# Six modulation pieces of four columns in place of twelve of two, in the attention of an encoder layer

## The chip, the cores and the metric

The kernel runs on one core of a Trainium2 chip. The metric is the device time of one execution, in microseconds (us); lower is better. PE is the matmul engine, PEld its weight load, DVE the vector engine, ACT the scalar engine, POOL the GpSimd engine; SP only issues DMAs.

## The reference

One encoder layer on x (1024 tokens, 1024 features), float32. A vector c conditions it:

```python
mod = (silu(c) @ w_ada + b_ada)            # 1024 -> 6 * 1024
sh1, sc1, g1, sh2, sc2, g2 = split(mod, 6)
h = rmsnorm(x, norm_g[0]) * (1 + sc1) + sh1
y = hybrid_mixer(h, ...)                   # three attentions A, B, C; 24 gates; output projection
x = x + g1 * rmsnorm(y, norm_g[1])
h = rmsnorm(x, norm_g[2]) * (1 + sc2) + sh2
x = x + g2 * rmsnorm(conv_ffn(h), norm_g[3])
```

The mixer has four heads for each of A (chunked), B (forgetting) and C (sparse, the best 256 keys of an indexer). Each attention's result is projected to 1024 features and multiplied by a sigmoid gate, `sigmoid(h @ w_in[:, gate columns] + b_gate)`, before the sum.

## The kernel before, in words

`mod` is kept as 48 columns of 128 values. Columns 0 to 15 (sh1, sc1) are made at the start, 40 to 47 (g2) at the end; the change touches neither. Columns 16 to 39 (g1, sh2, sc2) are first used when the attention is over; they are made meanwhile, in *pieces*.

A piece of two columns (`ada_load`, `ada_piece`): two DMAs (line 185) bring 1024 x 256 weights in two blocks of 512 KB. DVE makes c-weighted sums of the eight 128x256 slices into `ada_acc`, in two accumulators that take turns (2 instructions of line 196, 6 of line 198). POOL adds the two accumulators (line 204). PE sums over the partitions, one fp32 matmul of width 1 for each column (line 208; the trace shows each as two), into a PSUM bank of tag `d`. DVE makes two columns of `mod` out of the bank (line 210). `ada_acc` has one buffer.

The attention (lines 842 to 940) is a loop over 12 heads, each of four groups of two query blocks: PE makes scores, DVE adds a bias and takes maxima (line 762), ACT takes exponentials (772), POOL scales by the reciprocals of the sums (777), PE transposes (811), ACT and DVE split the result (816, 817), PE weighs the values (800, 801). Beside it, DVE and ACT search the thresholds of C's keys: 31 rounds of counting (`select_keys`, 647 to 668), and after them the masks (691 to 698), which C's first head needs.

The gates and pieces are *filler* for PE: `items` is a list that `tick` advances while the attention is written down, at a priority 100 lower. A gate (`m_tile`) loads 512 KB of weights (line 238, a `raw` buffer), splits them into a high and a low part (231 on ACT, 232 on POOL), runs 48 matmuls (247 to 249) into two banks of tag `d`, and evacuates each by ACT (530). There are two `d` banks, for gates and pieces alike, three `raw` buffers (`N_RAW`) of 512 KB for the weights of gates and of pieces, and four buffers for split weights, enough for two gates. 20 of the 24 gates are items; `ADA_AT` says behind which of them a piece stands. `run_all` calls the loads of item n+1 just before the steps of item n.

Nobody writes the order of the attention by hand: a planner simulates the engines' times and puts the instructions into each engine's queue by priority and readiness, past the written order where buffers allow. On the chip each engine then goes through its queue in that order.

Of the kernel before, what the change touches and what calls it, by code (L numbers as in the profile page):

```python
# [7 lines left out]
F32 = mybir.dt.float32  # L8
# [4 lines left out]
OP = mybir.AluOpType  # L13
# [3 lines left out]
P = 128  # L17
S = 1024
D = 1024
KD = D // P  # L20
# [10 lines left out]
HAND_FROM = 11  # L31
N_HELD = 2
LATE_M = (1, 3, 5, 7)
ADA_AT = (1, 2, 3, 4, 5, 6, 7, 8, 11, 13, 15, 17)
RELOAD = (1, 3, 5)
BB = "s"
N_F4 = 2
# [23 lines left out]
def encoder_layer(ctx: ExitStack, tc: tile.TileContext, x, w_ada, w_in, w_branch, w_out, w_up, w_down,  # L61
                  vec_a, vec_c, rel_pad, b_forget, cos_t, sin_t, out):
    nc = tc.nc
    act = nc.scalar
    dve = nc.vector
    pool = nc.gpsimd
    pe = nc.tensor
# [7 lines left out]
    small = ctx.enter_context(tc.tile_pool(name="small", bufs=4))  # L75
# [16 lines left out]
    def raw4(name, shape=(P, 1024), dt=F32):  # L92
        return rawp.tile(list(shape), dt, tag="raw", name=name, bufs=N_RAW)
# [13 lines left out]
    def bank(tag, name):  # L107
        return psum.tile([P, HALF], F32, tag=tag, name=name, bufs=N_BANKS[tag])
# [33 lines left out]
    one = const.tile([P, 1], F32, name="one")  # L142
# [19 lines left out]
    c_act = const.tile([P, KD], F32, name="c_act")  # L162
# [5 lines left out]
    mod = const.tile([P, 48], F32, name="mod")  # L168
    mod_b1 = const.tile([P, 48], F32, name="mod_b1")
# [3 lines left out]
    mod_g = const.tile([P, 48], F32, name="mod_g")  # L173
# [4 lines left out]
    def ada_load(srcs, alloc):  # L178

        wv = w_ada.rearrange("(k p) c -> p k c", p=P)  # L180
        raw = [alloc(f"ada_raw{g}", (P, 4, 2, P)) for g in range(2)]
        for g in range(2):
            ks_ = slice(4 * g, 4 * g + 4)
            if srcs[1] == srcs[0] + 1:
                nc.sync.dma_start(raw[g].rearrange("p k t c -> p k (t c)"), wv[:, ks_, srcs[0] * P:(srcs[0] + 2) * P])
            else:
                for j, u in enumerate(srcs):
                    nc.sync.dma_start(raw[g][:, :, j, :], wv[:, ks_, u * P:(u + 1) * P])
        return [raw[k // 4][:, k % 4] for k in range(KD)]

    def ada_steps(per_k):

        acc = small.tile([P, 2, 2, P], F32, tag="ada_acc", name="ada_acc", bufs=1)
        for k in range(KD):
            if k < 2:
                dve.tensor_scalar(acc[:, k], per_k[k], c_act[:, k:k + 1], None, op0=OP.mult)
            else:
                dve.scalar_tensor_tensor(acc[:, k % 2], per_k[k], c_act[:, k:k + 1], acc[:, k % 2],  # L198
                                         op0=OP.mult, op1=OP.add)
            yield acc  # L200

    def ada_end(srcs, acc, tag="n", eng=pool, pm=None):

        eng.tensor_tensor(acc[:, 0], acc[:, 0], acc[:, 1], op=OP.add)
        if pm is None:
            pm = bank(tag, "ada_ps")
        for j, t in enumerate(srcs):
            pe.matmul(pm[:, j:j + 1], acc[:, 0, j], one, start=True, stop=True)
        for j, t in enumerate(srcs):
            last = dve.scalar_tensor_tensor(mod[:, t:t + 1], pm[:, j:j + 1], mod_b1[:, t:t + 1],  # L210
                                            mod_g[:, t:t + 1], op0=OP.add, op1=OP.mult)
        return last

    def ada_piece(srcs, per_k, tag="n", pm=None):
        for acc in ada_steps(per_k):
            pass
        ada_end(srcs, acc, tag, pool, pm)
# [122 lines left out]
    with tc.manual_schedule(engines={E.Activation, E.DVE, E.Pool, E.PE}):  # L340
# [15 lines left out]
        for k in range(KD):  # L356
# [3 lines left out]
            if k + 1 < KD:  # L360
                g0_turn(k + 1, 0)
                steps = ada_steps(ada_in[k + 1])
# [75 lines left out]
    for hf in range(2):  # L438
        ts_ = slice(hf * HALF, (hf + 1) * HALF)
        pm = bank("n", f"pm2_{hf}")  # L440
# [98 lines left out]
    def early_gate(i):  # L539
        return gate(early[i] // KD, early[i] % KD, lambda tg: nc.sync.dma_start(gate_spill[i], tg), f4)  # L540
# [21 lines left out]
    need_B0 = len(items)  # L562
    items += z_AB(z_B, C_QB, C_KB, 1, "B")
    need_B2 = len(items)
    ada_todo = [(a, a + 1) for v in (2, 3, 4) for a in range(v * 8, v * 8 + 8, 2)]

    def ada_item(srcs):
        def steps(w):
            ada_piece(srcs, w, "d")
            yield  # L570
        return lambda: ada_load(srcs, raw4), steps

    for i in range(len(early)):
        items.append(early_gate(i))
        if i in ADA_AT:
            items.append(ada_item(ada_todo.pop(0)))
# [23 lines left out]
    for h in range(4):  # L600
        q_idx = q_next
        for b in range(NB - 1, 1, -1):
            n = P * (b + 1)
            w_h = wi[:, b, h:h + 1]
            for c0 in range(0, n, HALF):
                w = min(HALF, n - c0)
# [364 lines left out]
    for b in range(3):  # L971
# [5 lines left out]
        for m in range(KD):  # L977
# [12 lines left out]
            for hf in range(2):  # L990
# [7 lines left out]
                dst = M[m] if b == 0 else tg  # L998
# [483 lines left out]
    acc = hp.tile([P, NB, S], F32, tag="h", name="acc")  # L1482
# [267 lines left out]
```

## Time and profile before

| | us |
|---|---|
| median of three runs | 1585.77 |
| lowest, highest | 1585.55, 1587.79 |
| the profiled execution | 1589.77 |
| its span, first to last instruction | 1588.0 |
| PE busy in it | 1495.3 |
| DVE busy in it | 1179.6 |
| mean granted PE clock, of full speed | 0.987 |

The profiled execution is one run with the profiler on; views and terms below refer to its span. "Busy" is the time in which at least one instruction runs on the engine. PEclk is the granted clock: 1.00 is 2.4 GHz, 0.50 is 1.2 GHz. In a timeline an `xN` row merges N like instructions into one length. An arrow `<-` in a wait names the instruction that ended it.

The attention lies between about 195 and 700 us of the span; the pieces' instructions on DVE run from 297 to 646 us.

### The profile page before, as it was taken

Reading aid. Unit: us, or ns where it says so; the run is one execution under the profiler, and the core shown is the slowest. Engines: PE = TensorE matmul, PEld = TensorE weight load, DVE = VectorE, ACT = ScalarE, POOL = GpSimd, SP = SyncE. Lnnn points to the kernel's source line nnn. Section 1 sums busy time; section 2 is a strip of 40 time slices with the busy share of each in tenths; the row PEclk is TensorE's granted clock in tenths of the full one; section 3 lists DMA queues with packets and bytes.
Section 4 is the critical chain, followed back from the end, with each engine's and each line's share of the span. In section 5 each row is a group of like instructions: output and inputs, shape, how many; then the busy total and the mean of one; then the engine's idle time right before and its main releaser. Section 6 shows DMA issues by size and latency. Waiting matters only on the chain.

```text
span 1588.0 us, 21237 instructions
## 1 busy us (share of the span) xinstructions
PE 1495.3 (94%) x7322; PEld 1236.2 (78%) x7322; DVE 1179.6 (74%) x2166; ACT 786.0 (49%) x1462; POOL 564.0 (36%) x408
## 2 busy tenths in 40 slices
PE   3989999989998999989999989999999999999997
PEld 2768888777886888777788778788888887888885
DVE  6765888999669855556635678888778787778868
ACT  4434598886554445542234455555555555522222
POOL 3531544433443544203541233322222222423305
PEclk9989999999999999999999999999999999999998
DMA  9541333423444332336567322444444445898762
GB/s 282 139 107 34 112 108 86 153 80 121 160 146 123 99 124 87 110 134 198 185 251 259 130 81 93 146 146 155 158 149 165 153 152 171 340 361 292 278 226 106
DMA packets 187871, 253.98 MB, mean 160 GB/s; under 512 B 14891, under 2 KB 145139, under 8 KB 187763
## 3 DMA queue, kind: packets, MB, share of 16 engines
q1 hardware_dynamic: 187763, 252.62, 47.8%
q8 instruction: 58, 0.95, 0.3%
q14 instruction: 50, 0.41, 0.1%
HBM read 169.75 MB, written 74.97 MB: 154 GB/s over the span
## 4 chain that ended last, share of the span: by engine, by line
PE 69%; DVE 17%; issue 4%; ACT 4%; DMA 3%; POOL 1%; SPq 1%; DVEq 0%; POOLq 0%; ACTq 0%
PE X L1246 4%; PE X L1247 4%; PE X L1248 4%; PE g L247 4%; PE g L248 4%; PE g L249 4%; PE X L1610 2%; PE X L1611 2%; PE X L1612 2%; DVE junk L649 2%; PE V L1246 2%; PE V L1247 2%; PE V L1248 2%; DVE ada_acc L198 2%; PE V L1610 2%
## 5 line engine op out<-in xcount | busy, mean ns | idle before, releaser
L647 ACT ACTIVATE junk<-sc,thr 128x512 bf16<-128x512 f32 (+2 forms) x93 | 80.1, 862 | 30.0 <-DVE thr L668 25.0
L649 DVE TENSOR_SCALAR_CACHE_REDUCE junk<-sc,thr 128x384 bf16<-128x384 f32 (+2 forms) x93 | 89.6, 964 | 1.8
L1212 POOL TENSOR_TENSOR T<-ua 128x512 f32<-128x512 f32 x21 | 27.2, 1294 | 175.1 <-DVE rT L1198 165.5
L198 DVE SCALAR_TENSOR_TENSOR ada_acc<-ada_raw,c_act,ada_acc 128x256 f32<-128x256 f32 x120 | 79.4, 707 | 2.6 <-DMA ada_raw<-in_w_ada 2.5
L1290 POOL TENSOR_TENSOR cv<-cv,g 128x1024 f32<-128x1024 f32 x22 | 57.2, 2598 | 49.5 <-ACT cv L1289 45.3
L1247 PE MATMUL X<-left_S,rT 128*128 128x512 f32 (+1 forms) x184 | 70.8, 385 | 0.2 <-DVE left_S L1092 0.2
L1246 PE MATMUL X<-left_S,rT 128*128 128x512 f32 (+1 forms) x184 | 70.8, 385 | 0.0
L1248 PE MATMUL X<-left_S,rT 128*128 128x512 f32 (+1 forms) x184 | 70.7, 384 | 0.0
L1500 ACT ACTIVATE T<-work 128x512 fp32r<-128x512 f32 x40 | 25.0, 631 | 63.2 <-PE V L1612 26.0
L1213 POOL TENSOR_TENSOR ug<-ug 128x512 f32<-128x512 f32 x22 | 32.6, 1480 | 65.8 <-DVE ua L1206 65.8
L1621 DVE TENSOR_TENSOR acc<-acc,X 128x512 f32<-128x512 f32 x68 | 45.8, 682 | 13.7 <-PE X L1612 13.3
L1001 POOL TENSOR_TENSOR M<-M,tgb 128x1024 f32<-128x1024 f32 x12 | 30.6, 2548 | 69.2 <-DVE tgb L999 58.5
L1611 PE MATMUL X<-T,ring 128*128 128x512 f32 x120 | 47.0, 392 | 0.0
L1621 DVE TENSOR_TENSOR acc<-acc,V 128x512 f32<-128x512 f32 x56 | 37.2, 682 | 12.8 <-PE V L1612 12.5
L1612 PE MATMUL X<-T,ring 128*128 128x512 f32 x120 | 46.7, 390 | 0.0
L1610 PE MATMUL X<-T,ring 128*128 128x512 f32 x120 | 46.2, 393 | 0.0
L1198 DVE TENSOR_TENSOR rT<-ua,rT 128x512 fp32r<-128x512 f32 x45 | 39.1, 869 | 9.3 <-ACT rT L1197 8.9
L1197 ACT ACTIVATE rT<-ua 128x512 fp32r<-128x512 f32 x45 | 28.2, 627 | 34.7 <-DVE ua L1210 22.9
L1198 DVE TENSOR_TENSOR rB<-ua,rB 128x512 fp32r<-128x512 f32 x44 | 41.0, 935 | 2.0 <-ACT rB L1197 0.9
L1247 PEld LDWEIGHTS X<-left_S,rT 128*128 128x128 f32 x184 | 34.5, 187 | 8.0 <-DVE left_S L1092 0.4
L615 DVE SCALAR_TENSOR_TENSOR sc<-rl,wi,sc 128x512 f32<-128x512 f32 (+3 forms) x30 | 30.2, 1038 | 14.0 <-ACT rl L614 14.0
L1248 PEld LDWEIGHTS X<-left_S,rT 128*128 128x128 f32 x184 | 34.4, 187 | 7.7
(982 smaller groups left out, 5553.3 us busy)
## 6 DMA issues: line engine op xcount, KB each, us to landing
ring<-L_spill SPq DMA_DIRECT2D x70, 512.0 KB, 6.0
L_spill<-S SPq DMA_DIRECT2D x40, 512.0 KB, 4.1
L_spill<-A SPq DMA_DIRECT2D x30, 512.0 KB, 3.1
raw_g<-in_w_in SPq DMA_DIRECT2D x24, 512.0 KB, 4.3
ada_raw<-in_w_ada SPq DMA_DIRECT2D x24, 512.0 KB, 3.9
ua<-in_w_up SPq DMA_DIRECT2D x22, 512.0 KB, 4.3
ug<-in_w_up SPq DMA_DIRECT2D x22, 512.0 KB, 3.9
gate_spill<-tg SPq DMA_DIRECT2D x20, 512.0 KB, 2.6
```

The costliest lines, as they stand in the source:

```text
L198: dve.scalar_tensor_tensor(acc[:, k % 2], per_k[k], c_act[:, k:k + 1], acc[:, k % 2], op0=OP.mult, op1=OP.add)
L247: pe.matmul(o, wh[:, k], hh[:, k, ts_], start=(k == 0), stop=False)
L647: act.activation(junk_a[:, 0:n], scores[b], AF.Sign, scale=-1.0, bias=t_f, accum_out=cnt[:, j:j + 1])
L649: dve.tensor_scalar(junk_d[:, 0:n], scores[b], t_f, None, op0=OP.is_lt, op1=OP.add, accum_out=cnt[:, j:j + 1])
L1198: eng.tensor_tensor(hl_[1], src, hl_[0].bitcast(F32), op=OP.subtract)
L1246: pe.matmul(oc, r[:, 0, k], lh, start=(first and k == 0), stop=False, skip_group_check=True)
L1247: pe.matmul(oc, r[:, 0, k], ll, start=False, stop=False, skip_group_check=True)
L1248: pe.matmul(oc, r[:, 1, k], lh, start=False, stop=(last and k == 3), skip_group_check=True)
L1610: pe.matmul(o, lh, r[:, 0], start=(starts and k == 0), stop=False, skip_group_check=True)
L1611: pe.matmul(o, lh, r[:, 1], start=False, stop=False, skip_group_check=True)
L1612: pe.matmul(o, ll, r[:, 0], start=False, stop=(k == 1), skip_group_check=True)
L1621: dve.tensor_tensor(dst, dst, banks[i], op=OP.add)
```

## The change

Six pieces of four columns replace twelve of two. `ADA_AT` becomes (4, 7, 10, 13, 15, 17): no piece behind gates 1 to 3, 5, 6, 8 and 11 any more. A piece now loads four blocks of two 128x512 slices, three of them ahead of its steps (in all three `raw` buffers), the fourth from inside, between the second and the third slice. It has one accumulator of 128x512: one instruction of the kind of line 196 and seven of the kind of line 198, each of which reads what the one before wrote. POOL's addition is gone. Four matmuls of width 1 follow, and then two instructions on DVE for all four columns: the first adds the bank and `mod_b1`, the second multiplies by `mod_g` in place. Bytes loaded, DMAs (24) and PE's matmuls (24 columns) stay what they were.

```diff
-ADA_AT = (1, 2, 3, 4, 5, 6, 7, 8, 11, 13, 15, 17)
+ADA_AT = (4, 7, 10, 13, 15, 17)
...
-    ada_todo = [(a, a + 1) for v in (2, 3, 4) for a in range(v * 8, v * 8 + 8, 2)]
-
-    def ada_item(srcs):
-        def steps(w):
-            ada_piece(srcs, w, "d")
-            yield
-        return lambda: ada_load(srcs, raw4), steps
+    ada_todo = [a for v in (2, 3, 4) for a in (v * 8, v * 8 + 4)]
+
+    def ada_item(a):
+
+        wv = w_ada.rearrange("(k p) c -> p k c", p=P)
+
+        def load(g):
+            raw = raw4(f"ada_row{a}_{g}", (P, 2, 4 * P))
+            nc.sync.dma_start(raw, wv[:, 2 * g:2 * g + 2, a * P:(a + 4) * P])
+            return raw
+
+        def steps(raws):
+            acc = small.tile([P, 4 * P], F32, tag="ada_acc", name=f"ada_acc{a}", bufs=1)
+            for k in range(KD):
+                if k == 2:
+                    raws.append(load(3))
+                s_ = c_act[:, k:k + 1]
+                if k == 0:
+                    dve.tensor_scalar(acc, raws[0][:, 0], s_, None, op0=OP.mult)
+                else:
+                    dve.scalar_tensor_tensor(acc, raws[k // 2][:, k % 2], s_, acc, op0=OP.mult, op1=OP.add)
+            pm = bank("d", "ada_ps")
+            for j in range(4):
+                pe.matmul(pm[:, j:j + 1], acc[:, j * P:(j + 1) * P], one, start=True, stop=True)
+            dst = mod[:, a:a + 4]
+            dve.tensor_tensor(dst, pm[:, 0:4], mod_b1[:, a:a + 4], op=OP.add)
+            dve.tensor_tensor(dst, dst, mod_g[:, a:a + 4], op=OP.mult)
+            yield
+        return lambda: [load(g) for g in range(3)], steps
```

## Rows read from the trace of the kernel before

**Rows 1.** Page, busy time: each engine, its share of the span, instructions.
```profile
PE 1495.3 (94%) x7322; PEld 1236.2 (78%) x7322; DVE 1179.6 (74%) x2166; ACT 786.0 (49%) x1462; POOL 564.0 (36%) x408
```

**Rows 2.** Stretches of the attention: length, busy time of each engine, PEclk, DMA.
```profile
280.00:400.00 120.00, 110.36 (x562) 91.20 (x560) 116.13 (x300) 90.72 (x196) 46.56 (x42) 0.97 0.38 121
...
484.00:545.00 61.00, 53.06 (x282) 44.73 (x280) 55.58 (x100) 24.44 (x47) 25.86 (x17) 0.94 0.29 88
545.00:680.00 135.00, 130.96 (x735) 111.10 (x735) 73.38 (x207) 71.26 (x145) 52.83 (x47) 1.00 0.33 106
355.00:365.00 10.00, 8.01 (x31) 6.60 (x32) 9.90 (x21) 7.18 (x13) 6.68 (x5) 0.83 0.30 90
489.00:503.00 14.00, 8.06 (x28) 6.32 (x29) 13.46 (x22) 4.43 (x9) 6.51 (x4) 0.76 0.34 113
```

**Rows 3.** Waits of PE, 280 to 400 us: total, times, longest.
```profile
PE g L247 <- DVE mod L210: 2.6, 2, 1.9
PE A3s L426 <- DVE A3m L762: 1.7, 2, 0.9
...
PE A2y L801 <- DVE A2pl L817: 1.0, 1, 1.0
```

**Rows 4.** Waits of PE, 400 to 680 us.
```profile
PE g L247 <- DVE mod L210: 6.9, 2, 5.4
```

**Rows 5.** Timeline, 489 to 503 us: start, length, engine, line.
```profile
492.30 3.55 DVE L196 TENSOR_SCALAR ada_acc<-ada_raw,c_act 128x256 f32<-128x256 f32 x2
495.77 0.33 DVE L210 SCALAR_TENSOR_TENSOR mod<-ada_ps,mod_b,mod_g 128x1 f32<-128x1 f32 x2
...
493.32 2.37 POOL L232 TENSOR_TENSOR wg_2l<-raw_g,wg_2h 128x1024 fp32r<-128x1024 f32 x1
...
496.15 0.79 PE L247 MATMUL g<-hh,wg_1h 128*128 128x512 f32 x1 [5.42 <-DVE mod L210]
```

**Rows 6.** Groups of instructions by line, 280 to 660 us, the pieces' own.
```profile
L198 DVE SCALAR_TENSOR_TENSOR ada_acc<-ada_raw,c_act,ada_acc 128x256 f32<-128x256 f32 x72 | 50.3, 731 | 0.1
...
L196 DVE TENSOR_SCALAR ada_acc<-ada_raw,c_act 128x256 f32<-128x256 f32 x24 | 20.1, 861 | 0.0
...
L210 DVE SCALAR_TENSOR_TENSOR mod<-ada_ps,mod_b,mod_g 128x1 f32<-128x1 f32 x24 | 4.1, 207 | 0.6 <-PE ada_ps L208 0.5
...
L204 POOL TENSOR_TENSOR ada_acc<-ada_acc 128x256 f32<-128x256 f32 x12 | 9.3, 774 | 20.9 <-DVE ada_acc L198 13.7 <-DVE hit L665 6.9 <-DVE B2ri L776 0.4
```

**Rows 7.** Tile ada_acc, 280 to 660 us: nanoseconds min/median/max.
```profile
L198 DVE SCALAR_TENSOR_TENSOR ada_acc<-ada_raw,c_act,ada_acc x72: 455/475/2631, 298.6 to 617.3; 128x256 f32<-128x256 f32 x72
...
L196 DVE TENSOR_SCALAR ada_acc<-ada_raw,c_act x24: 334/349/2565, 297.2 to 611.0; 128x256 f32<-128x256 f32 x24
```

**Rows 8.** Timeline of DVE around 449 and 1330 us.
```profile
449.30 0.61 DVE L196 TENSOR_SCALAR ada_acc<-ada_raw,c_act 128x256 f32<-128x256 f32 x2
...
450.03 2.06 DVE L198 SCALAR_TENSOR_TENSOR ada_acc<-ada_raw,c_act,ada_acc 128x256 f32<-128x256 f32 x5
...
1329.89 1.39 DVE L1286 SCALAR_TENSOR_TENSOR cv<-a,ccol,cv 128x1023 f32<-128x1023 f32 x1 [0.47 <-ACT cv L1285]
1331.31 1.28 DVE L1287 SCALAR_TENSOR_TENSOR cv<-a,ccol,cv 128x1022 f32<-128x1022 f32 x1
```

**Rows 9.** Groups by line and form: 128x512 and 128x1024 in SBUF.
```profile
L1601 DVE SCALAR_TENSOR_TENSOR xf<-work,n_3r,xf 128x512 f32<-128x512 f32 x2 | 1.4, 740 | 0.0
...
L1116 DVE TENSOR_SCALAR xn<-x,n_3r 128x1024 f32<-128x1024 f32 x1 | 0.7, 745 | 0.0
```

**Rows 10.** Waits of the DMA queue, 280 to 660 us.
```profile
SPq L238 <- DVE ada_acc L198: 30.6, 7, 13.7
```

**Rows 11.** Loads of line 185: issue to landing.
```profile
DMA to landing us min/median/max: 3.5/4.3/10.0
```

**Rows 12.** Timeline: a piece ready, and its matmuls.
```profile
385.49 0.74 POOL L204 TENSOR_TENSOR ada_acc<-ada_acc 128x256 f32<-128x256 f32 x1 [6.87 <-DVE hit L665]
...
388.63 0.50 PE L208 MATMUL ada_ps<-one,ada_acc 128*128 128x1 f32 x4
```

## The prediction

> **What bounds the kernel now.** I read the page first: PE is busy for 94% of the span, DVE for 74% [rows 1]. So only what makes PE stand still, or run at half clock, can move the time by much; DVE's work counts where PE waits for it. Then the windows of the attention [rows 2]. From 280 to 400 us DVE is busy for 116.1 of 120 us and PE stands for 9.6. From 484 to 545 us, where the masks of C are made, DVE is busy for 55.6 of 61 and PE stands for 7.9. From 545 us on DVE has room (73.4 of 135) and PE hardly stands (4.0). Then the waits of PE: the first in both lists is the same, the first matmul of a gate (line 247) waiting for `mod` (line 210): 2.6 us in two waits before 400 us [rows 3], 6.9 us in two behind it [rows 4]. That is 9.5 us in four waits, from twelve pieces.
>
> The timeline shows how the longest comes about [rows 5]. The piece's matmuls are done, its bank is the next one for the gate, and DVE has only to make the two columns of `mod` (0.33 us). But its queue holds the first two sums of the *next* piece before that, and these take 3.55 us, because POOL is splitting weights (493.32, 2.37 us) and they end about when POOL ends. PE starts at 496.15, 5.42 us late, and then at a lower clock: 0.76 over 489 to 503 us [rows 2]. The same from 355 to 365 us: 0.83, behind a wait of 1.9 us [rows 2, 3].
>
> **What the change costs and saves, part by part.** *DVE's work.* Before, a sum over 128x256 takes 0.475 us at the median, but its mean is 0.731; the first kind takes 0.349 against a mean of 0.861; the longest are 2.6 us [rows 6, 7], the length of a POOL operation. Undisturbed, a piece of two columns needs little: five sums in 2.06 us are a step of (2.06 - 0.475) / 4 = 0.40; the two first ones take 0.61, a step of 0.26 [rows 8]; `mod` 0.33 [rows 5]. So 2 x 0.26 + 6 x 0.40 + 0.33 = 3.25, for twelve 39 us. The trace has 50.3 + 20.1 + 4.1 = 74.5 [rows 6], of which some 7 us (96 x 0.07) are overlap of neighbours: about 68, so 29 us are waiting for POOL.
>
> After: a sum over 128x512 with SBUF on both sides takes 0.74 [rows 9]. Each reads what the one before wrote; the pair of lines 1286 and 1287 is such a pair, and the second starts 0.03 us after the first has ended [rows 8], where the pieces' own sums start 0.07 before it. A step is thus 0.77. The first kind takes 0.35 at 256 wide and 0.745 at 1024 [rows 7, 9], about 0.48 at 512. Two small instructions, 0.2 each by line 210 [rows 6]. So 0.48 + 7 x 0.77 + 0.4 = 6.3, for six 38 us: the same as the 39 before. Wider instructions save nothing in themselves, because the single accumulator gives up what the two had. The waiting for POOL is not shown for this form: if it goes with the length of the chain it stays 29 us, if with the number of instructions (48 for 96) it is 14.5. The 2.6 us maxima are one POOL operation each, which speaks for the number; I take 18, so DVE gets 11 + 1 = 12 us back, at least 1 and at most 15.
>
> By the Trainium skill, VectorE: DVE Perf Modes, section The DRAIN you can't avoid, the next DVE instruction does not issue before the pipe is empty, and a semaphore between chained ones costs nothing extra. By that the step after would be no longer than with two accumulators, and DVE would get some 42 x 0.1 = 4 us more back; the rows above show otherwise, and I go by them.
>
> *POOL's twelve additions* (0.774 us each, 9.3 in all [rows 6]) go. POOL is busy for 46.6 of 120 us [rows 2] and nothing here hangs on it: 0 for PE; what they cost DVE is in the term above. *DMAs*: as many and as large. *PE's matmuls*: as many. *Six fewer steps of filler*: 0.
>
> *Waits for `mod`.* Twelve hand-overs of a `d` bank from a piece to a gate become six. In four of twelve PE waited; nothing makes the remaining six longer: the bank is free after one DVE instruction in place of two, and the next piece is two or three gates away, so its first sums no longer stand in front. So I halve: 9.5 / 2 = -4.8 us. Bounds 0 and -9.5.
>
> *The clock behind these waits.* Lost now: (1 - 0.83) x 10 = 1.7 and (1 - 0.76) x 14 = 3.4 us [rows 2], together 5.1. Halved as well: -2.5. Bounds 0 and -5.1.
>
> *The stretch from 280 to 400 us.* It loses the pieces behind gates 1 to 3; with piece 4 still at its end some 17 us of DVE work go, of 116. The largest waits of PE for DVE there beside `mod` are 1.7 and 1.0 [rows 3]. Most of that goes: -2. Bounds 0 and -2.7.
>
> *The stretch from 484 to 545 us* gets a piece twice as long in a DVE that is full: 6.3 - 3.25 = 3.1 us of work more. Half of it covered by gates on PE: +1.5. Bounds 0 and +3.1. The pieces behind gates 13, 15 and 17 also double, where DVE is busy for 73.4 of 135 us [rows 2]: 0. If that cover were gone, they would cost 3 x 3.1 = 9 us.
>
> Sum: -4.8 - 2.5 - 2 + 1.5 = -7.8 us. The profiled execution takes 1589.8, 4.0 above the median of the three runs; 1589.8 - 7.8 = 1582.0 there, and **1585.8 - 7.8 = 1578.0 at the median**. With the bounds the forecast's own range is 1569 to 1583. What a measurement here can tell from no change is about 0.2%, 3.2 us.
>
> **The rivals.** *No change that can be measured.* The hand-overs get fewer, but each piece has twice the chain, and PE's waits per column stay: the first three terms shrink to -2 in all, the fourth stays +1.5: 1585. For it: the 5.42 us hang on POOL's operations and DVE's full queue, which remain [rows 5]. Against it: in three of the four waits (at 357, 495 and 546 us) the next piece's first sums stand in DVE's queue around `mod`, as in [rows 5], and that pattern goes.
>
> *Slower: the fourth block.* A piece takes all three `raw` buffers; its fourth block can only be asked for when DVE has read the first two slices, behind the next gate's weights. A load takes 4.3 us, up to 10.0 [rows 11], and the queue already waits 30.6 us, in seven waits of up to 13.7, for a piece's sums to free a buffer [rows 10]. If the planner lets DVE reach the seventh slice before the block has landed, DVE stands, in order, and everything behind it: PE's wait can then be like the longest today, 5.4 + 3.4 of clock = 8.8 us. One such piece takes back the 7.8 us of the sum, 1586.8; two of six give 1585.8 - 7.8 + 17.6 = 1595.6. So it decides from the second on. Against it: a piece's sums are ready before its matmuls are due, by 2.4 us in the tightest case (386.23 to 388.63 [rows 12]) with a piece behind each gate; with two or three gates between them there is more room.
>
> *No change: the masks.* The long piece in the full stretch from 484 to 545 us is put before the masks, and C's first head starts later by all of it, 6.3 us and one spell of low clock, 3.4: 1585.8 - 7.8 + 9.7 = 1587.7, no change either. For it: DVE is full there. Against it: filler stands 100 lower in priority.
>
> That the planner orders everything behind 280 us anew adds some us of either sign to each case.
>
> By the Trainium skill, SBUF — State Buffer, section Who interferes with whom, a DVE instruction with two SBUF inputs and a GpSimd instruction that reads SBUF exclude each other for a whole instruction, the second one waits. The trace agrees: 3.55 us for two sums of 0.35 beside POOL's 2.37 [rows 5]. By that rule the second of the two new small instructions (both inputs in SBUF) can wait where line 210, with its bank in PSUM, didn't; the bank is free by then, so PE doesn't see it.
>
> **How the numbers follow.** Forecast 0.57; no change by waits 0.15; by the masks 0.08; the fourth block 0.20. Faster by over 0.2% only in the first, 0.57; same in the next two, 0.23; slower in the last, 0.20. The range for 8 in 10: below, the forecast's bound, 1569; above, through both cases of no change and half way from one late block to two, 1592. What is left out is the rest of the fourth block, and a little below.
>
> **What would show it.** Right: about six groups of seven 128x512 sums on DVE, near 0.74 us at the median, step 0.77; in PE's waits line 247 behind `mod` at 5 us or less; DVE below 105 of 120 us from 280 to 400; PE's clock above 0.9 in all stretches of the attention. Wrong: waits of DVE for the load of `ada_row`, waits of PE for `ada_acc`, PE standing for more than 8 us from 484 to 545, or a PE wait of more than 3 us that the trace of before doesn't have.

## The result

| | before | after |
|---|---|---|
| median (us) | 1586.78 (four runs, 1585.55 to 1590.38) | 1577.39 (four runs, 1574.61 to 1578.40) |
| ratio, 95% interval | | 0.993 [0.9911, 0.995] |
| profiled execution | 1589.77 | 1577.21 |

By the ratio of the table the change makes the kernel 0.7% faster; the medians differ by 9.4 us, which is 0.6%, and the interval holds both. The forecast was 1578.0.

The page of the kernel after answers to [rows 1]. DVE is busy for 22.5 us less, PE for 2.0.

```profile
span 1575.4 us, 21143 instructions
...
PE 1493.3 (95%) x7322; PEld 1234.4 (78%) x7322; DVE 1157.1 (73%) x2106; ACT 787.0 (50%) x1462; POOL 559.6 (36%) x396
```

The windows of after, for the first three stretches of [rows 2]: length, busy time of each engine, PEclk, DMA share, GB/s. DVE's load from 280 to 400 us falls from 116.1 to 105.9 us; PE stands there for 6.4 us instead of 9.6, and from 484 to 545 us for 4.3 instead of 7.9.

```profile
280.00:400.00 120.00, 113.63 (x612) 94.98 (x610) 105.86 (x276) 97.23 (x204) 51.97 (x43) 1.00 0.41 129
...
484.00:545.00 61.00, 56.74 (x292) 46.86 (x291) 53.88 (x103) 26.50 (x53) 27.93 (x19) 0.94 0.29 87
545.00:680.00 135.00, 131.76 (x741) 110.61 (x740) 73.53 (x198) 69.30 (x140) 44.92 (x39) 1.00 0.34 113
```

A fixed time does not hold the same work in two kernels, so the difference is placed by events. A begins with the first score of A0, B, C and the merge of the gated results follow, and the end is the first transposition of a row of `mod` behind the merge. Before, the four stages and their sum:

```profile
197.80:355.10 157.30, 148.03 (x877) 126.79 (x875) 145.33 (x398) 136.76 (x304) 66.12 (x60) 1.00 0.35 108
355.10:552.10 197.00, 182.93 (x984) 154.94 (x985) 163.47 (x377) 103.12 (x202) 88.53 (x69) 0.97 0.41 127
552.10:700.80 148.70, 144.18 (x819) 122.03 (x817) 77.10 (x216) 77.15 (x155) 50.07 (x46) 1.00 0.32 103
700.80:822.40 121.60, 114.79 (x481) 91.96 (x482) 67.31 (x84) 32.47 (x51) 50.08 (x20) 0.97 0.60 207
197.80:822.40 624.60, 589.93 (x3159) 495.72 (x3158) 453.22 (x1071) 349.51 (x711) 254.81 (x194) 0.98 0.41 132
```

After:

```profile
194.00:347.70 153.70, 148.59 (x883) 128.02 (x881) 141.65 (x392) 136.55 (x303) 65.67 (x59) 1.00 0.35 107
347.70:539.50 191.80, 180.19 (x971) 151.58 (x970) 145.31 (x322) 104.02 (x204) 81.79 (x60) 0.97 0.41 123
539.50:691.10 151.60, 146.46 (x829) 122.76 (x827) 81.80 (x216) 76.93 (x155) 49.73 (x44) 1.00 0.35 115
691.10:809.70 118.60, 112.89 (x481) 90.78 (x481) 66.04 (x84) 32.56 (x51) 50.19 (x20) 0.99 0.62 212
194.00:809.70 615.70, 588.13 (x3159) 493.14 (x3157) 434.80 (x1011) 350.06 (x711) 247.37 (x182) 0.99 0.42 134
```

The stretch is 8.9 us shorter: A -3.6, B -5.2, C +2.9, merge -3.0. PE has the same matmuls in both, so a longer busy time points to a lower granted clock. Standing (length less busy) goes from 34.7 to 27.6 us, busy time from 589.9 to 588.1. The other 3.8 us of the two spans lie ahead of it (A begins at 197.8 and 194.0) and are not the change's: in the profiles of this study A begins anywhere from 194.0 to 200.0 us.

The waits of PE in after, 280 to 700 us, the three longest. No line there has line 247 behind `mod` any more ([rows 3, 4]: 9.5 us). PE now waits longer for DVE's score maxima (line 784 is line 762 of before): 9.0 us in these three, 10.5 in all, where before has 3.3.

```profile
PE B0s L426 <- DVE B0m L784: 3.3, 2, 1.7
PE B3s L426 <- DVE B3m L784: 3.0, 4, 1.3
PE Bb L888 <- DVE B2m L784: 2.7, 1, 2.7
```

The pieces' instructions of after on DVE, from the groups of 280 to 660 us, then four sums in a row in DVE's timeline and the lengths of the sums (least, median, longest). They answer to [rows 6, 7, 8].

```profile
L585 DVE SCALAR_TENSOR_TENSOR ada_acc<-ada_row,c_act,ada_acc 128x512 f32<-128x512 f32 x42 | 39.3, 936 | 12.9 <-DMA ada_row<-in_w_ada 12.4
L583 DVE TENSOR_SCALAR ada_acc<-ada_row,c_act 128x512 f32<-128x512 f32 x6 | 4.8, 796 | 1.8 <-PE ada_ps L588 1.8
L591 DVE TENSOR_TENSOR mod<-mod,mod_g 128x4 f32<-128x4 f32 x6 | 3.5, 580 | 0.0
L590 DVE TENSOR_TENSOR mod<-ada_ps,mod_b 128x4 f32<-128x4 f32 x6 | 0.9, 157 | 1.8 <-PE ada_ps L588 1.8
```

```profile
407.15 3.12 DVE L585 SCALAR_TENSOR_TENSOR ada_acc<-ada_row,c_act,ada_acc 128x512 f32<-128x512 f32 x4 [2.03 <-DMA ada_row<-in_w_ada]
```

```profile
L585 DVE SCALAR_TENSOR_TENSOR ada_acc<-ada_row,c_act,ada_acc x42: 725/752/2777, 339.6 to 612.0; 128x512 f32<-128x512 f32 x42
```

Together 48.5 us against 74.5 before. A step of the chain is (3.12 - 0.752) / 3 = 0.79.

Two stretches of DVE's timeline in after show what stands around a hand-over now.

```profile
452.93 0.48 DVE L583 TENSOR_SCALAR ada_acc<-ada_row,c_act 128x512 f32<-128x512 f32 x1 [1.81 <-PE ada_ps L588]
453.33 0.15 DVE L590 TENSOR_TENSOR mod<-ada_ps,mod_b 128x4 f32<-128x4 f32 x1
453.45 2.78 DVE L585 SCALAR_TENSOR_TENSOR ada_acc<-ada_row,c_act,ada_acc 128x512 f32<-128x512 f32 x1
...
519.82 0.47 DVE L583 TENSOR_SCALAR ada_acc<-ada_row,c_act 128x512 f32<-128x512 f32 x1
520.22 0.15 DVE L590 TENSOR_TENSOR mod<-ada_ps,mod_b 128x4 f32<-128x4 f32 x1
```

The next piece's first sum stands in front of `mod` still, at 453 and at 520 us, with 0.48 and 0.47 us. At 520 the matmuls of the piece had been done since 512.3 (eight at 511.37, 0.95 us), and the bank stayed taken for 8 us, nearly all of it for masks and maxima in DVE's queue. PE's waits have no gate that stood for that bank.

Other waits of after do lie behind a piece's sums. PE's two waits for B0's maxima, in order of time:

```profile
354.13 2.38 POOL L412 TENSOR_TENSOR Bq<-z_Bq_back,Bq 64x1024 fp32r<-64x1024 f32 x1
354.31 2.74 DVE L585 SCALAR_TENSOR_TENSOR ada_acc<-ada_row,c_act,ada_acc 128x512 f32<-128x512 f32 x1
356.98 0.28 DVE L784 CUSTOM_DVE_ANT_0 B0e<-B0s,nb 128x128 f32<-128x128 f32 x1
357.32 0.50 PE L426 MATMUL B0s<-Bk,Bq 128*128 128x512 f32 x1 [1.71 <-DVE B0m L784]
...
362.13 0.75 DVE L585 SCALAR_TENSOR_TENSOR ada_acc<-ada_row,c_act,ada_acc 128x512 f32<-128x512 f32 x1 [1.43 <-DMA ada_row<-in_w_ada]
...
365.59 0.42 DVE L784 CUSTOM_DVE_ANT_0 B0e<-B0s,nb 128x256 f32<-128x256 f32 x1
366.07 0.50 PE L426 MATMUL B0s<-Bk,Bq 128*128 128x512 f32 x1 [1.61 <-DVE B0m L784]
```

In the first a sum, 2.74 us long beside POOL instead of 0.75, stands right in front of the maxima. In the second DVE has stood for 1.43 us for the piece's seventh slice, the first of its fourth block, and the maxima come behind that block's sums.

Low clock in after's attention, by the windows with the lowest: 0.79 over 8 us and 0.66 over 10 us, (1 - 0.79) x 8 + (1 - 0.66) x 10 = 5.1 us. The same sum over the two spells that the prediction has of before gave 5.1.

```profile
474.00:482.00 8.00, 5.31 (x29) 4.28 (x29) 7.37 (x14) 2.69 (x4) 2.48 (x2) 0.79 1.06 254
512.00:522.00 10.00, 7.77 (x30) 6.50 (x31) 9.94 (x21) 4.73 (x9) 5.08 (x3) 0.66 0.32 105
```

Each kernel has a third spell of 1.7 us: before at 388 us, (1 - 0.81) x 9, and after at 690 us, (1 - 0.66) x 5, on the border to the merge.

```profile
388.00:397.00 9.00, 7.76 (x32) 5.84 (x31) 9.00 (x25) 4.25 (x9) 5.07 (x5) 0.81 0.21 77
...
690.00:695.00 5.00, 4.36 (x13) 3.39 (x14) 1.33 (x4) 1.52 (x4) 0.00 (x0) 0.66 0.82 278
```

### The profile page after: what moved, and what is told of

It is laid out like the page before. It is cut to its first block, busy times and chain, and to the rows that moved or that the text cites. A ratio compares the mean times of both kernels' runs of the same rounds, so it can differ in the third digit from the quotient of the medians.

```text
span 1575.4 us, 21143 instructions
## 1 busy us (share of the span) xinstructions
PE 1493.3 (95%) x7322; PEld 1234.4 (78%) x7322; DVE 1157.1 (73%) x2106; ACT 787.0 (50%) x1462; POOL 559.6 (36%) x396
## 4 chain that ended last, share of the span: by engine, by line
PE 69%; DVE 15%; DMA 5%; issue 4%; ACT 4%; SPq 2%; POOL 1%; DVEq 0%; POOLq 0%; ACTq 0%
PE g L247 4%; PE g L248 4%; PE X L1268 4%; PE g L249 4%; PE X L1269 4%; PE X L1270 4%; PE X L1632 2%; PE X L1633 2%; PE X L1634 2%; PE V L1268 2%; PE V L1269 2%; PE V L1270 2%; PE V L1632 2%; PE V L1633 2%; PE V L1634 2%
## 5 line engine op out<-in xcount | busy, mean ns | idle before, releaser
L1522 ACT ACTIVATE T<-work 128x512 fp32r<-128x512 f32 x40 | 25.0, 631 | 63.2 <-PE V L1634 26.1
L585 DVE SCALAR_TENSOR_TENSOR ada_acc<-ada_row,c_act,ada_acc 128x512 f32<-128x512 f32 x42 | 39.3, 936 | 12.9 <-DMA ada_row<-in_w_ada 12.4
```

## The experiments

The change does three things at once: half as many pieces, each in another form, and other places for them. The theory of the prediction is that the number of hand-overs of a `d` bank counts. The rivals are that the places count, and that DVE's work counts wherever it stands. Ratios are to the kernel before, timed beside it on the same chip; "stretch" is the one above, of one profile each. e1 to e4, e5 to e8 and e9 to e12 are three occasions, and after's own ratio is of a fourth.

| | ratio [95%] | stretch | PE stands | DVE busy, 280 to 400 |
|---|---|---|---|---|
| before | 1 | 624.6 | 34.7 | 116.1 |
| after | 0.9930 [0.9911, 0.9950] | 615.7 | 27.6 | 105.9 |
| e1 two columns, places of after | 1.0095 [1.0072, 1.0117] | 644.6 | 42.1 | 107.2 |
| e2 four columns, early places | 0.9946 [0.9929, 0.9963] | 612.5 | 28.8 | 111.4 |
| e3 no pieces | 0.9816 [0.9797, 0.9836] | 594.0 | 18.7 | 102.2 |
| e4 four columns, later places | 0.9990 [0.9977, 1.0003] | 622.1 | 33.7 | 106.6 |
| e5 before, bank emptied by ACT | 1.0009 [0.9995, 1.0023] | 626.9 | 35.7 | 113.4 |
| e6 after, bank emptied by ACT | 0.9981 [0.9966, 0.9996] | 623.4 | 31.2 | 107.9 |
| e7 e4, bank emptied by ACT | 0.9928 [0.9910, 0.9945] | 611.4 | 24.9 | 107.2 |
| e8 e2, bank emptied by ACT | 0.9925 [0.9909, 0.9941] | 611.5 | 25.7 | 111.9 |
| e9 two columns, spread | 0.9895 [0.9880, 0.9909] | 609.4 | 26.5 | 107.1 |
| e10 after, two hand-overs each | 0.9959 [0.9944, 0.9973] | 617.9 | 30.5 | 109.2 |
| e11 before, 2 of 8 sums | 0.9927 [0.9914, 0.9941] | 613.8 | 26.1 | 105.9 |
| e12 four columns, places between | 0.9934 [0.9920, 0.9947] | 611.2 | 26.3 | 106.4 |

**e1: the places alone, in pairs.** The pieces of before, two behind each gate behind which after has one.

```diff
-ADA_AT = (1, 2, 3, 4, 5, 6, 7, 8, 11, 13, 15, 17)
+ADA_AT = (4, 4, 7, 7, 10, 10, 13, 13, 15, 15, 17, 17)
```

> The form of before (pieces of two columns, two accumulators, an addition on POOL), at the places of after: two such pieces one behind the other behind gates 4, 7, 10, 13, 15 and 17. Twelve hand-overs of a bank, none of them early. If the number of hand-overs makes the gain, the time stays near before, 1583 to 1588 us, and line 247 still waits 5 us or more for mod. If the place makes it, the time is that of after, 1575 to 1580, and these waits are gone.

Slower by 0.95%. The longest wait of PE is new:

```profile
PE ada_ps L208 <- POOL ada_acc L204: 6.3, 1, 6.3
```

There is one `ada_acc`, so the second of a pair can't begin before the first is through. That is 6.3 of a stretch 20.0 us longer: PE stands for 7.4 us more in all and is busy for 12.6 us more with the same matmuls, at a granted clock of 0.96 against 0.98:

```profile
198.90:843.50 644.60, 602.54 (x3158) 507.24 (x3157) 446.37 (x1071) 351.03 (x711) 259.95 (x194) 0.96 0.40 128
```

Neither expected range came out: pieces back to back are worse than single ones at the places of before and at those of e9. The places of after are thus no gain for this form in pairs; e9 asks the same without pairs.

**e2: the number alone.** Six pieces of after, four of them within the first eight gates: as many columns early as before.

```diff
-ADA_AT = (4, 7, 10, 13, 15, 17)
+ADA_AT = (2, 4, 6, 8, 13, 17)
```

> The form of after (six pieces of four columns), spread like the pieces of before: behind gates 2, 4, 6, 8, 13 and 17. If the number of hand-overs makes the gain, most of it stays: 1576 to 1581 us. If the place makes it (DVE is full from 280 to 400 us), the time is near before, 1583 to 1588, with DVE again busy for 113 us or more of the 120 from 280 to 400.

It keeps most of the gain near the old places, with DVE at 111.4 of 120 us. With as many columns early, the form and its smaller number bring a gain; which of the two does, this run does not tell.

**e3: no pieces.** `ADA_AT` is empty, and columns 16 to 39 of `mod` are set to 1 instead of being computed.

```diff
-ADA_AT = (1, 2, 3, 4, 5, 6, 7, 8, 11, 13, 15, 17)
+ADA_AT = ()
...
+    dve.memset(mod[:, 16:40], 1.0)
```

> Left out: all twelve pieces of the attention; columns 16 to 39 of mod are set to 1 instead. What is missing against before is all that the pieces can cost. By the terms of the prediction: 9.5 us of waits, 5.1 of clock, 2.7 of the early stretch and some 5 us of PE (48 short matmuls of about 0.11 us), 22 us: 1564. After should then lie between this and before. If after is within 4 us of this one, there is nothing left to gain in the pieces; if the time is near 1577, after has taken all of it already.

```profile
199.30:793.30 594.00, 575.27 (x3111) 483.64 (x3110) 390.39 (x951) 349.73 (x711) 243.67 (x182) 1.00 0.36 117
```

This is what there is to win: 1591.01 - 1561.29 = 29.7 us for all twelve pieces, more than the 22 us of the expectation; the change takes 9.4. PE still stands for 18.7 us with the attention and the gates alone, at full clock throughout, and DVE is still busy for 102.2 of the 120 us.

**e4: after, every early piece one gate later.**

```diff
-ADA_AT = (4, 7, 10, 13, 15, 17)
+ADA_AT = (5, 8, 11, 13, 15, 17)
```

> After, with the first three pieces one gate later: behind gates 5, 8, 11, 13, 15 and 17. All that the prediction reasons with is unchanged, so by it the time is that of after within 2 us, 1575 to 1580. If the gain is a matter of how the planner happens to order the instructions, the time differs from after by 4 us or more.

The gain is gone, with six hand-overs and the first pieces late. By the condition set ahead of the run, 4 us or more from after, the gain hangs on the order that the planner finds. One hand-over accounts for most of the loss; from the timeline:

```profile
532.65 5.96 POOL L412 TENSOR_TENSOR Cq<-z_qc,Cq 64x1024 fp32r<-64x1024 f32 x2
...
534.19 2.22 DVE L720 TENSOR_SCALAR sc<-junk 128x1024 f32<-128x1024 bf16 x1
...
537.00 1.90 DVE L583 TENSOR_SCALAR ada_acc<-ada_row,c_act 128x512 f32<-128x512 f32 x1
...
538.82 0.15 DVE L590 TENSOR_TENSOR mod<-ada_ps,mod_b 128x4 f32<-128x4 f32 x1
...
539.12 0.77 PE L247 MATMUL g<-hh,wg_4h 128*128 128x512 f32 x1 [5.72 <-DVE mod L590]
```

It is [rows 5] again, in the new form, but the next piece's first sum, drawn out beside POOL, is only 1.90 us of it. In front of that DVE's queue has 2.22 us of the masks (line 720) and two maxima of 0.68 and 0.74. A stand of 5.72 us and, in the window around it, low clock, (1 - 0.74) x 13 = 3.4 us:

```profile
533.00:546.00 13.00, 7.28 (x25) 5.84 (x25) 12.46 (x19) 4.16 (x8) 8.02 (x4) 0.74 0.53 163
```

Together 9.1 us, about as much as the whole change brings.

**e5 to e8: the bank emptied by ACT.** Before, after, e4 and e2, where the sums leave the bank on ACT, so that DVE's queue no longer holds it. The edit of e6 (e7 and e8 have it too; e5 copies two columns in the same way and makes `mod` from the copy):

```diff
-            dve.tensor_tensor(dst, pm[:, 0:4], mod_b1[:, a:a + 4], op=OP.add)
+            act.activation(dst, pm[:, 0:4], AF.Copy)
+            dve.tensor_tensor(dst, dst, mod_b1[:, a:a + 4], op=OP.add)
```

> Before, with one thing changed: ACT copies the piece's two columns out of the bank, and DVE makes mod from the copy, so that the bank no longer waits for DVE. Twelve pieces at their places, the sums on DVE as they are. If the gain of the change comes from DVE being late at fewer hand-overs, the waits of line 247 for mod (9.5 us) and the two spells of low clock behind them (5.1 us) go: 1.0 to 0.7 per cent below before. If it comes from DVE's load or from the form of the sums, the time stays within 0.2 per cent of before.

> After, with the bank emptied by ACT instead of DVE. After has no wait of line 247 for mod left, so by the theory of the hand-overs little is to be had: within 0.3 per cent of after, 0.4 to 0.9 per cent below before. More than that would mean that late hand-overs still cost something that shows under another name, as the 8 us by which DVE is late at 512 us.

> The shifted places (5, 8, 11, 13, 15, 17), which stayed at the time of before, with the bank emptied by ACT. Its one wait for mod is 5.7 us and the spell of low clock behind it 6.8 us long. If that one late hand-over is what the shift lost, the ratio to before falls from 0.999 to 0.993 or 0.994, that of after. If the shift lost it by another order of the planner, it stays at 0.997 or above.

> Four-column pieces behind gates 2, 4, 6, 8, 13 and 17 with the bank emptied by ACT. The places alone gave 0.9946 with no wait for mod in the profile, so the theory of the hand-overs expects no more: 0.993 to 0.996.

In e5 the wait for `mod` has left the list, and the time is what it was: other waits took its place (2.8 us for B3's maxima, 2.7 for A3's, 2.0 of a gate for ACT's evacuation of a gate). In e6 it costs after most of its gain, against the expectation of no change; in e7 it gives e4 all of after's gain, as expected; in e8 it changes little. So the wait for `mod` is not itself the price of a piece. Where it is one long stand, as in e4, taking it away went with a gain; in e5 PE waited for something else of DVE's. Each of the four is ordered anew by the planner, so that e7's gain is the hand-over's alone is likely but not shown.

**e9: the places alone, one by one.** The pieces of before, twelve hand-overs, four pieces instead of eight within the first eight gates.

```diff
-ADA_AT = (1, 2, 3, 4, 5, 6, 7, 8, 11, 13, 15, 17)
+ADA_AT = (4, 5, 7, 8, 10, 11, 12, 13, 14, 15, 16, 17)
```

> The form of before (twelve pieces of two columns), later: one piece behind each of the gates 4, 5, 7, 8, 10, 11, 12, 13, 14, 15, 16 and 17. DVE is relieved between 280 and 400 us as in after, the hand-overs stay twelve. If the number of pieces makes the gain, the ratio to before is 0.997 to 1.003. If the place makes it, it is near 0.993.

The fastest of all kernels that compute everything, by 1.05% against before, and beyond the 0.993 expected for the place. Its stages:

```profile
199.50:354.30 154.80, 148.00 (x879) 127.37 (x878) 142.77 (x394) 137.22 (x304) 65.89 (x60) 1.00 0.34 106
354.30:535.40 181.10, 172.11 (x941) 146.38 (x942) 143.75 (x340) 101.91 (x202) 86.45 (x66) 0.98 0.39 121
535.40:687.30 151.90, 149.10 (x859) 128.06 (x857) 97.97 (x255) 78.91 (x157) 55.27 (x50) 1.00 0.37 125
687.30:808.90 121.60, 113.64 (x480) 91.15 (x481) 66.41 (x84) 32.59 (x51) 50.14 (x20) 0.97 0.59 207
```

A and B together take 335.9 us against 354.3 before and 345.5 after; C takes 3.2 us more than before, with DVE at 98.0 of 151.9 us. Some 40 matmuls, about 9 us of PE by estimate, have moved from B to C (941 and 859 against 984 and 819), so the whole stretch, 15.2 us shorter, says more than its parts. PE has no wait for `mod`, with as many hand-overs as before.

**e10: after, with as many hand-overs as before.** Each piece's four columns go through the bank in two halves, the second behind the next gate.

```diff
-            for j in range(4):
-                pe.matmul(pm[:, j:j + 1], acc[:, j * P:(j + 1) * P], one, start=True, stop=True)
+            for j in range(2):
+                pe.matmul(pm[:, j:j + 1], acc[:, (c + j) * P:(c + j + 1) * P], one, start=True, stop=True)
...
+        def second(_):
+            hand_over(kept[0], 2)
...
+        if i - 1 in ADA_AT:
+            items.append(half)
```

> After, with each piece's four columns handed over in two halves: two of them behind the piece's gate, the other two behind the next gate, each half through a bank of its own. Sums and places are those of after, hand-overs are twelve. If the hand-overs make the difference, the time goes back to that of before (0.998 to 1.002), with line 247 waiting 5 us or more for mod. If the sums make it (wider instructions, no addition on POOL, fewer waits for POOL), it stays at 0.992 to 0.996.

It keeps 0.41%, with one wait for `mod` of 1.1 us. Its interval overlaps that of after, so six further hand-overs cost 0.3% or nothing that can be told. The second half also holds `ada_acc` until the next gate, so the edit is not of the hand-overs alone.

**e11: before, with the hand-overs and a quarter of the sums.** Six of the eight sums of each piece are left out, so `mod` lacks them; POOL's addition, the bank and `mod`'s line remain.

```diff
-            ada_piece(srcs, w, "d")
+            for k in (0, 7):
+                dve.tensor_scalar(acc[:, k % 2], w[k], c_act[:, k:k + 1], None, op0=OP.mult)
+            ada_end(srcs, acc, "d")
```

> Left out: six of the eight sums of each of the twelve pieces of before (two instructions of the kind of line 196 remain, so these columns of mod are wrong). Loads, the addition on POOL, the matmuls and the twelve hand-overs stay, at the places of before. If what DVE has to do for the sums makes the losses, most of the way to the run without pieces is covered: 0.984 to 0.989. If the hand-overs in themselves make them, 5 us or more of waits for mod remain and the ratio is 0.994 to 1.000.

With twelve hand-overs at the places of before, leaving out three quarters of the sums gives as much as the change, 0.73%, and PE's waits for `mod` fall to one of 1.5 us. Neither expected range came out: the gain is far from the 1.84% of e3, so most of what the pieces cost lies in the rest of them or in the order. The weights' buffers also come free earlier here, so it is not DVE's work alone that is less.

**e12: another set of places for after.**

```diff
-ADA_AT = (4, 7, 10, 13, 15, 17)
+ADA_AT = (3, 6, 9, 12, 15, 17)
```

> After with the first four pieces one gate earlier: behind gates 3, 6, 9, 12, 15 and 17. It is one more sample of the form at other places. So far the form gave 0.993, 0.9946 and 0.999 with DVE's hand-over. If the form gains by itself and the planner's order only scatters it, this lies between 0.992 and 0.999, and PE's lost time (standing and low clock) tells where.

As after. Of four sets of places for the same form three gain 0.5 to 0.7% and one, e4, nothing.

## Why the prediction came out

The time was right to 0.6 us, and the sign; as a difference the forecast was 7.8 us and the medians show 9.4. The parts were not right, so the fit of the sum is in part luck. Against the forecast, in the stretch: waits for `mod` -4.7 and the merge -3.0, the clock +2.5 and other waits +4.0, together -1.2.

- **DVE's work.** The floor holds: a step is 0.79 us, forecast 0.77. The waiting for POOL was mis-sized: six undisturbed pieces need 38 us, the groups have 48.5, so some 10 us are waiting, against 18 taken and a lower bound of 14.5. DVE got 74.5 - 48.5 = 26.0 us of instruction time back, where the forecast in the same measure was 18.5 (74.5 - 56). Overlaps counted once, it is 22.5 by the page, where the forecast was 12.
- **Waits for `mod`**: -9.5 us, forecast -4.8; all four went. The reason given for it, that "the next piece is two or three gates away, so its first sums no longer stand in front", is wrong: one stands in front at 453 and 520 us, and in e4 it is 1.90 us of a stand of 5.72. Nor is it the number: e9 has no such wait with twelve hand-overs, and of the four placements of the new form three have none and e4 has one. That after is among the three is luck of its order.
- **The clock**: -2.5 forecast. Three spells went and three came, 6.8 us either way; PE's busy time in A, B and C together is 475.1 before and 475.2 after.
- **Other waits of the attention.** PE stands 6.0 us less in A, B and C (27.9 to 21.9), so with -9.5 for `mod`, waits of 3.5 us came elsewhere, those for B's maxima above all. The forecast had -2 and +1.5 for its two stretches.
- **The merge**: -3.0, not forecast. Its waits of PE for ACT's `wb` fall from 3.7 us to 1.9 and its granted clock goes from 0.97 to 0.99. e9 has the stage at 121.6, as before, so it belongs to one order or the other; what decides it stays open.
- **The rival of no change by waits** held what e5 and e4 show: waits that are taken away come back under another name, and in e4 the whole of the gain goes. It lost here; at one of four placements of the form it would have won.
- **The rival of the fourth block**: its mechanism came, at a small size. DVE stands for the loads, 12.4 us in all, which the prediction had named as a sign of being wrong. No wait of PE names a piece's sums, but at 366 us PE waits 1.61 us for maxima that come behind DVE's 1.43 us for a fourth block. The longest stands of DVE for loads, 3.49 and 2.03 us from 405 to 415 us, have no wait of PE behind them. **The masks** are not seen: C takes 2.9 us longer, and no wait of PE for them is in the list. **The signs**: of those for being right, DVE below 105 us was just missed (105.9).

What carries the gain? Not the number of hand-overs by itself: e9 and e10 have twelve and gain 1.05% and 0.41%, e4 has six and gains nothing, e5 frees the bank early and gains nothing. What is left is that less of the pieces' work on DVE where DVE is full means fewer and shorter waits of PE: thinning it by place (e9), by number and form (e2) or by leaving sums out (e11) brings 0.5 to 1.1% each, and none at all 1.8% (e3). This is argued, not shown. e1, e4 and e6 don't fit it without their own late waits, and DVE's busy time from 280 to 400 us doesn't order the runs: 107.2 in e1 and 106.6 in e4, which gain nothing, 111.4 in e2, which does. The change thins by place and by form at once, and its form is not needed for the gain: the old form at spread places (e9) is ahead of it. e9 and after were timed on different occasions and their intervals just part; e9 against e12, the same form as after and timed beside it, parts clearly (0.9895 [0.9880, 0.9909], 0.9934 [0.9920, 0.9947]).

Open stays how much of each difference is the order that the planner happens to find. e4 and e6 are small edits of after and 0.5 to 0.6% slower; e4's loss is read mostly from one hand-over; e6's has no single place (2.8 us for B2's maxima, 3.4 for `wb`, five spells of lower clock) and stays open. A difference of 0.3% between two placements is not explained by any of this.

## What to carry to other kernels

Filler that uses a second engine needs room on that engine, not only on PE: read DVE's share of each stretch before choosing places, and spread the filler singly (e9 against e1). Where a planner makes the order, try several placements of the same form, since here one late hand-over cost about as much as the whole change brings; and where taking one wait away gives nothing, look for the engine behind all of them. Behind a named wait, look at everything that stood in that engine's queue, not only at the last instruction. Compare two traces from a common event, not from the start of the span.

## What was not expected of the hardware

A tiny instruction can take far longer than its size shows. Line 591 (128x4, both inputs in SBUF) takes 0.580 us in the mean, but that is one of 2.36 us and five of 0.15 to 0.52. The long one ends when a POOL operation beside it ends:

```profile
599.81 2.63 POOL L232 TENSOR_TENSOR wg_2l<-raw_g,wg_2h 128x1024 fp32r<-128x1024 f32 x1 [1.07 <-ACT wg_2h L231]
...
600.10 2.36 DVE L591 TENSOR_TENSOR mod<-mod,mod_g 128x4 f32<-128x4 f32 x1
```

Line 590 (the same size, one input in PSUM) takes 0.15 to 0.16 all six times, at 453.33 us beside a POOL operation too. By the Trainium skill, SBUF — State Buffer, section Who interferes with whom, a DVE instruction with two SBUF inputs contends with a GpSimd instruction that reads SBUF, and one with at most one SBUF input does not, outside the modes in which DVE uses both of its ports. The two lines agree with it. The prediction's row for this rule [rows 5] is of line 196, which has one tensor and a column of `c` as inputs; the sum at 354.31 us above, with two tensors, is a case of it.

Not every stand of PE lowers the granted clock, and the length of a single one doesn't tell. From 355 to 370 us PE of after stands for 1.71 and 1.61 us and the clock stays at 1.00; from 474 to 482 us, with one stand of 2.69, it is 0.79, and from 512 to 522 us, with stands of 0.91 and 1.33, it is 0.66.

```profile
355.00:370.00 15.00, 11.57 (x65) 9.04 (x64) 13.27 (x34) 8.25 (x19) 2.40 (x4) 1.00 0.26 74
```
